# Layer trunk of gated DeltaNet and GLA on one core: the recurrence's output and the gate computed transposed

## The chip, the core and the metric

One core of one Trainium2 chip runs the whole program. The metric is device time in microseconds (us), the median of several executions. The kernel before took 3088.72 us, the median of three runs (3087.71 to 3092.79).

## What is computed

Two layers over 2048 tokens of width 1024, all in float32. Layer one is a gated DeltaNet with 8 heads (key width 128, value width 256), layer two gated linear attention (GLA) with 4 heads of the same widths. In both, an input projection gives q, k, v and a gate; a recurrence over the tokens gives an output o for each head, which is normalised, gated and projected back:

```python
def gated_rmsnorm(o, w, gate):
    o = o * lax.rsqrt(jnp.mean(o * o, -1, keepdims=True) + RMS_EPS)
    return o * w * jax.nn.silu(gate)

def l2norm(t):
    return t * lax.rsqrt(jnp.sum(t * t, -1, keepdims=True) + L2_EPS)

# layer one: q, k, v pass a causal convolution of 4 taps and SiLU, then q and k pass l2norm
#   S_t = exp(g_t) S_{t-1} (I - beta_t k_t k_t^T) + beta_t v_t k_t^T ;  o_t = S_t q_t
# layer two:
#   S_t = diag(exp(gk_t)) S_{t-1} + k_t^T v_t ;  o_t = q_t S_t
# both:
#   x = layer_norm(ALPHA * x + gated_rmsnorm(o, norm_w, gate) @ w_out)
```

## The kernel before

The tokens come in 4 groups of 512 (`TG`), a group in 4 chunks of 128 (`NC`). A unit of work is one head of one layer over one group: 32 units of layer one and 16 of layer two, 48 in all, in the order of `PHASES`, which sets the second layer's groups between those of the first. Each unit goes through four stages.

`gemms` projects the group's x on the unit's columns: k and q (`kq`), values (`val`) and gate. Each operand is split in a rounded high part and the rest, and every product is made of three (`mm3`: high by high, high by low, low by high), over 8 blocks of 128 input channels. `by_channel` makes the weights stationary and moves 512 tokens; its result has channels on the partitions, two groups of 24 matmuls in PSUM. `by_token` makes 128 tokens stationary and moves the 256 weight columns; its result has tokens on the partitions, four groups of 24 matmuls. The groups are staggered by the `LAGS_C` and `LAGS_T` steps, so that their ends are spread. `kq`, and in layer one `val`, go by channel; the gate, and in layer two `val`, by token. A first head's gate weights carry 16 more columns, from which the decays come. Weight tiles (`wc`, 11 buffers) are loaded raw once (`wraw`, 5 buffers), split in high and low by ScalarE and GpSimd, kept in HBM, and loaded from there for later groups. The gate passes tanh on ScalarE and a product on VectorE into `sg`.

`preps` prepares the chunk matrices of the recurrence. In layer one (`gdn_prep`) k and q are transposed on TensorE, 4 transposes each, and ScalarE sums their squares from PSUM with an accumulator; q's norm is not applied to q but joins the output's norm later (`qn`).

`chains` runs the recurrence over the 4 chunks with the state `S`. For each chunk the output `do` (tokens by 256 values) is the sum of two products in PSUM; `output` squares it on ScalarE with an accumulator (`ssq`) and multiplies it by the gate into `og` on VectorE. At the end GpSimd raises `ssq` to the power -1/2 (`z`), and 8 transposes turn `og` so that values lie on the partitions, each bank of which is split in high and low parts (`oth`, `otl`).

`outs` multiplies these by the output weights, 8 banks of 6 matmuls of 512 columns, and VectorE adds each bank, times `z`, to the row of x (`y`); after a layer's last head comes the layer norm.

No engine order is written by hand. A recorder notes every operation, and `Recorder.place` lays all of them out ahead of time by costs per operation and by rank (recurrence first, then preparation, projection out, GEMM, layer norm); the order of each engine's queue is then fixed. PSUM has 8 banks: 3 for the GEMMs (`psg`), 3 for preparation and outputs (`psc`), one for the recurrence (`psh`) and one for the projection out (`pso`). Since a helper issues everything, all instructions have line 358, and a row is known by its tiles.

Of the kernel before, what the change touches and what calls it, by code (L numbers as in the profile page):

```python
# [16 lines left out]
P = 128  # L17
# [9 lines left out]
ALPHA = 4.0 ** 0.25  # L27
BIG = 1.0e30
NORM = 0.5 * DV ** 0.5 / ALPHA
LEVELS = (1, 2, 4, 8, 16, 32, 64)  # L30

C_ID, C_TRI, C_ONE, C_LO, C_UP, C_BLK, C_LV = 0, 1, 2, 3, 4, 5, 6
N_CST = C_LV + 5


def shape_constants(np):
    i = np.arange(P)[:, None]
    j = np.arange(P)[None, :]
    c = np.zeros((P, N_CST, P), np.float32)
    c[:, C_ID] = i == j  # L40
    c[:, C_TRI] = i <= j
    c[:, C_ONE] = 1.0
# [335 lines left out]
def trunk(ctx, tc, x, xT, w_in1, conv, a_log, dt_bias, nw1, w_out1, w_in2, gk_up, gk_b, nw2, w_out2,  # L378
# [54 lines left out]
    nws = [T(f"nw{k}", [P, 2]) for k in range(2)]  # L433
    gkb = T("gkb", [P, H2])
    mhalf = T("mhalf", [P, NC])
    up = T("up", [80, 512], dt=F32R)
    halo = T("halo", [P, 32, 3])
    S1 = [T(f"S1_{h}", [P, DV]) for h in range(H1)]
# [9 lines left out]
    def setup():  # L448
        sync.dma_start(nalog[:], a_log.unsqueeze(0).broadcast_to([P, H1]))
        sync.dma_start(dtb[:], dt_bias.unsqueeze(0).broadcast_to([P, H1]))  # L450
        sync.dma_start(cst[:].rearrange("p a b -> p (a b)"), consts)
        sync.dma_start(nws[0][:], nw1)
        v.tensor_scalar(nws[0][:], nws[0][:], NORM, None, ALU.mult)
        s.activation(nalog[:], nalog[:], AF.Exp)
        v.tensor_scalar(nalog[:], nalog[:], -1.0, None, ALU.mult)
        v.memset(mhalf[:], -0.5)
        v.tensor_reduce(id16[:], ident.rearrange("p (a b) -> p b a", b=16), mybir.AxisListType.X, ALU.add)
        for t in S1 + S2 + [halo]:
            v.memset(t[:], 0.0)
# [91 lines left out]
        return [(t[:, j, 0, :], t[:, j, 1, :]) for j in range(2)]  # L551

    def gemm(u, specs, group, lags, done):
        xs = u.G["x"]
        d, chunks = [None] * len(lags), {}
        for i in range(KC + lags[-1]):
            for a, lag in enumerate(lags):
# [5 lines left out]
                if a == 0:  # L563
# [40 lines left out]
    class Unit:  # L604
        def __init__(self, at, kind, gi, h):
            self.at, self.kind, self.gi, self.h = at, kind, gi, h
            self.t0 = gi * TG
            self.first, self.last = h == 0, h == (H1, H2)[kind] - 1

        def w_specs(self):  # L610
            h = self.h
            if self.kind == 0:
                gate = [(QKV + h * DV, DV, 0)] + ([(QKV + H1 * DV, 2 * H1, 0)] if self.first else [])
                kq = [(h * P, P, 1024)]
                val = [(2048 + h * DV, DV, 0)]
# [16 lines left out]
    def gemms(u):  # L632
# [11 lines left out]
            rec.rank = R_GEMM  # L644
        specs = u.w_specs()

        def gate(width):
            u.sg = T("sg", [P, NC, DV], 2)
            if u.first:
                u.G["low"] = T("ba", [P, NC, 16])  # L650

            def done(d, n):
                t = T("th", [P, 512], 2)
                s.activation(t[:, :DV], d[:, :DV], AF.Tanh, scale=0.5)
                if u.first:
                    s.copy(u.G["low"][:, n, :], d[:, DV:width])
                v.scalar_tensor_tensor(u.sg[:, n, :], t[:, :DV], 1.0, d[:, :DV], ALU.add, ALU.mult)
# [20 lines left out]
        if u.first and u.at:  # L678
            gate(DV + 16)
        u.kq = T("kq", [P, 2, NC, P], 2)  # L680
        gemm(u, specs["kq"], by_channel, LAGS_C, kq_done)
        if u.at == 0:
            gate(DV + 16)
        u.vt = T("vt", [P, NC, DV], 2)
        if u.kind == 0:
            gemm(u, specs["val"], by_channel, LAGS_C, val_done)
            rec.rank = R_PREP
# [7 lines left out]
        else:  # L695
# [15 lines left out]
    def gdn_logits(G, gi):  # L711
# [28 lines left out]
        mm(d[:, 1, :], C(C_ONE), zz)  # L740
# [9 lines left out]
        row = T("gcT", [H1 * NC, P])  # L750
        s.copy(row[:], dT)
        rows = T(f"gcT_{gi}", [H1 * NC, P], p=dr)
        acts.dma_start(rows[:], row[:])
        G.update(beta=beta, gc=gc, gdec=gl, eg=eg, rows=rows)

    def later_half(a, sz):
# [8 lines left out]
    def gdn_prep(u):  # L765
# [26 lines left out]
        rk = r[:]  # L792
        brk, br2, s1 = (small(k, NC) for k in ("brk", "br2", "s1"))
        v.tensor_scalar(qn[:], ss[:, NC:], 1e-6, P * DV * 1e-6, ALU.add, ALU.mult)
# [166 lines left out]
    def output(u, n, do, og, ssq):  # L961
        jk = T("junk", [P, DV], 1, BF16)
        s.activation(jk[:], do, AF.Square, accum_out=ssq[:, n:n + 1])
        v.tensor_tensor(og[:, n, :], do, u.sg[:, n, :], ALU.mult)

    def gdn_chain(u, og, ssq):
        S, p, kq = S1[u.h], u.prep, u.kq
        eg = u.G["eg"]
        for n in range(NC):
# [6 lines left out]
            mm(d, p["Uf"][:, n], Rt[:])  # L976
            wt = T("wt", [P, DV], 2)
            s.copy(wt[:], d)
            do = PS("c", [P, DV])
            mm(do, p["qd"][:, n], S[:], True, False)  # L980
# [3 lines left out]
            mm(do, p["Bt"][:, n], wt[:], False, True)  # L984
            output(u, n, do, og, ssq)

    def gla_chain(u, og, ssq):
        S, p = S2[u.h], u.prep
        for n in range(NC):
            d = PS("h", [P, DV])  # L990
            mm(d, p["kd"][:, n], u.vt[:, n, :])
            do = PS("c", [P, DV])
            mm(do, p["At"][:, n], u.vt[:, n, :], True, False)
            mm(do, p["qd"][:, n], S[:], False, True)
            v.scalar_tensor_tensor(S[:], S[:], p["el"][:, n:n + 1], d, ALU.mult, ALU.add)
            output(u, n, do, og, ssq)

    def chains(u):
        rec.rank = R_CHAIN
        og, ssq = T("og", [P, NC, DV], 1), small("ssq", NC)  # L1000
        (gdn_chain if u.kind == 0 else gla_chain)(u, og, ssq)
        z = small("z", NC)
        if u.kind == 1:
            rsqrt(z[:], ssq[:], DV * 1e-6)
        else:
            v.tensor_tensor(ssq[:], ssq[:], u.prep["qn"][:], ALU.add)
            rsqrt(z[:], ssq[:], 0.0)
        u.z = z
        u.oT = []
# [133 lines left out]
```

## Time and profile before

| | us |
|---|---|
| median of 3 runs | 3088.72 |
| the profiled execution | 3087.8 |
| its span, first to last instruction | 3086.0 |
| TensorE busy | 3009.3 |
| VectorE busy | 2051.1 |
| ScalarE busy | 1142.8 |
| GpSimd busy | 474.2 |

The mean granted TensorE clock was 0.995. A float32 product shows as two instructions, the three parts of a GEMM product as one each. Matmuls are pipelined: one lasts longer in the records than it holds back the next, so times are better read from one start to the next. Idle time of an engine is told with what ended it.

### The profile page before, as it was taken

The page shows a single profiled execution, that of the slowest core. Times are in us where ns is not written, and L with a number is a line of the kernel's source. Part 1 is how long each engine was busy: PE and PEld are TensorE (multiplying, and loading weights), DVE is VectorE, ACT ScalarE, POOL GpSimd, SP SyncE. Part 2 cuts the span into 40 slices and gives each one's busy share as a digit, 9 for nine tenths or more (in the row PEclk, how much of TensorE's full clock was granted, in tenths as well). Part 3 has the DMA queues.
Part 4 walks back from the last instruction along what each step waited for, and adds up shares of the span by engine and source line. Part 5 has one row for each costly group of instructions (what it writes and reads, how often), then busy time and mean ns, then how long its engine had stood idle before and what let it go on. Part 6 is the DMA issues. An engine that isn't in the chain of part 4 may idle for free. (4 is left out here: it accounts for less than half of the span.)

```text
span 3086.0 us, 51431 instructions
## 1 busy us (share of the span) xinstructions
PE 3009.3 (98%) x18430; PEld 2580.0 (84%) x18430; DVE 2051.1 (66%) x4810; ACT 1142.8 (37%) x3075; POOL 474.2 (15%) x820
## 2 busy tenths in 40 slices
PE   9999999999999999999999999999999999999997
PEld 7778888778888878988888888998888888889886
DVE  7777777866666685576675667447666667646645
ACT  5444445433223454433332344223333333422421
POOL 5433333510000232210000000001000000000000
PEclk9999999999999999999999999999999999999999
DMA  6565667764455567674445445547444544655542
GB/s 197 167 206 186 208 217 229 220 218 124 136 164 174 156 207 269 212 240 154 126 144 180 144 157 194 171 153 251 132 134 152 161 134 149 224 168 186 189 143 94
DMA packets 428272, 545.50 MB, mean 177 GB/s; under 512 B 38720, under 2 KB 364608, under 8 KB 415984
## 3 DMA queue, kind: packets, MB, share of 16 engines
q1 hardware_dynamic: 414000, 524.32, 54.1%
q10 hardware_dynamic: 14016, 17.90, 1.8%
q8 instruction: 145, 2.38, 0.3%
q14 instruction: 111, 0.91, 0.1%
HBM read 414.89 MB, written 127.21 MB: 176 GB/s over the span
## 5 line engine op out<-in xcount | busy, mean ns | idle before, releaser
L358 PE MATMUL psg<-xh,wc 128*128 128x512 f32 x2560 | 898.1, 414 | 6.4 <-ACT xh L358 2.8
L358 PE MATMUL psg<-wc,xh 128*128 128x256 f32 (+1 forms) x4096 | 807.4, 290 | 10.8 <-POOL wc L358 3.9
L358 PEld LDWEIGHTS psg<-wc,xh 128*128 128x128 f32 x4096 | 652.8, 189 | 36.5 <-POOL wc L358 5.6
L358 PE MATMUL psg<-wc,xl 128*128 128x256 f32 (+1 forms) x2048 | 586.7, 289 | 0.0
L358 PEld LDWEIGHTS psg<-xh,wc 128*128 128x128 f32 x2560 | 478.2, 189 | 104.3 <-ACT xh L358 3.9
L358 PE MATMUL psg<-xl,wc 128*128 128x512 f32 x1280 | 526.8, 412 | 0.1
L358 PE MATMUL pso<-wo,oth 128*128 128x512 f32 x1472 | 471.1, 400 | 6.0 <-DVE y L358 5.3
L358 DVE SCALAR_TENSOR_TENSOR y<-pso,z,y 128x512 f32<-128x512 f32 x368 | 274.6, 746 | 179.7 <-PE pso L358 175.4
L358 PEld LDWEIGHTS psg<-wc,xl 128*128 128x128 f32 x2048 | 386.8, 190 | 7.6
L358 POOL TENSOR_TENSOR wc<-wraw,wc 128x256 fp32r<-128x256 f32 (+1 forms) x336 | 278.1, 845 | 420.4 <-ACT wc L358 373.9
L358 DVE SCALAR_TENSOR_TENSOR acc<-pb,taps,acc 128x512 f32<-128x512 f32 x384 | 307.3, 802 | 51.7 <-ACT acc L358 44.1
L358 PEld LDWEIGHTS pso<-wo,oth 128*128 128x128 f32 x1472 | 258.0, 188 | 63.8 <-DVE y L358 17.1
L358 PE MATMUL pso<-wo,otl 128*128 128x512 f32 x736 | 293.1, 398 | 0.5 <-DVE otl L358 0.3
L358 PEld LDWEIGHTS psg<-xl,wc 128*128 128x128 f32 x1280 | 241.6, 189 | 48.4 <-DVE xl L358 1.9
L358 ACT ACTIVATE th<-psg 128x256 f32<-128x256 f32 (+1 forms) x256 | 108.2, 436 | 465.2 <-PE psg L358 434.6
L358 ACT ACTIVATE junk<-psc 128x128 bf16<-128x128 f32 (+1 forms) x448 | 144.6, 323 | 240.5 <-PE psc L358 135.2
L358 ACT COPY pb<-psg 128x512 f32<-128x512 f32 x128 | 74.9, 585 | 303.6 <-PE psg L358 279.4
L358 PEld LDWEIGHTS pso<-wo,otl 128*128 128x128 f32 x736 | 138.3, 188 | 32.1 <-DVE otl L358 2.0
L358 POOL COPY halo<-pb 128x3 f32<-128x3 f32 x128 | 29.9, 233 | 879.7 <-ACT pb L358 878.9
L358 DVE SCALAR_TENSOR_TENSOR sg<-th,psg 128x256 f32<-128x256 f32 x192 | 80.0, 417 | 127.6 <-ACT th L358 111.7
L358 ACT CAST wc<-wraw 128x256 fp32r<-128x256 f32 (+1 forms) x336 | 126.9, 407 | 90.7 <-DMA wraw<-in_w_in 77.4
L358 DVE SCALAR_TENSOR_TENSOR S<-S,eg,psh 128x256 f32<-128x256 f32 x128 | 61.1, 477 | 125.1 <-PE psh L358 124.4
(169 smaller groups left out, 4282.0 us busy)
## 6 DMA issues: line engine op xcount, KB each, us to landing
wc<-wk SPq DMA_DIRECT2D x776, 256.0 KB
wo<-wok SPq DMA_DIRECT2D x70, 1024.0 KB
wk<-wc SPq DMA_DIRECT2D x272, 256.0 KB
wraw<-in_w_in SPq DMA_DIRECT2D x336, 128.0 KB
wok<-wo SPq DMA_DIRECT2D x24, 1024.0 KB
Arep<-blk SPq DMA_DIRECT2D x32, 512.0 KB
woraw<-in_w_out SPq DMA_DIRECT2D x48, 256.0 KB
wc<-wk SPq DMA_DIRECT2D x40, 272.0 KB
```

What stands on the lines that cost most here:

```text
L358: tc.keep_in_program_order(op.call(*[real(a) for a in op.args], **{k: real(a) for k, a in op.kw.items()}))
```

## The change

The gate is computed by channel in all units but five (the first head of layer one in each group, and the very last unit, which keep the old form: `by_tok`). The output of the recurrence is computed with values on the partitions: for each of the two products of a chunk, the two halves of the value operand are stationary and the 128-token operand moves. The result, squared and gated, needs no transposing; `og` is split directly. The squares are kept whole (`sq`); the two halves are added, in layer one q's squares (scaled) are added to them, the sum is split, and two products with a matrix of ones give every partition the sum over all of them; a product with the identity and four accumulating copies bring the sums back to tokens on partitions. So q is no longer transposed for its norm. In layer two a first head computes its values first, with the 16 more columns, and the gate last. By-token groups with kept weights are computed in two passes of two chunks each, with the weights loaded for each pass. There is one weight buffer and one raw buffer fewer, and the matrix of ones is made on the chip.

```diff
-W_BUFS, RAW_BUFS, X_RAW_BUFS = 11, 5, 4
+W_BUFS, RAW_BUFS, X_RAW_BUFS = 10, 4, 4
...
+    ones = T("ones", [P, P], dt=F32R)
...
     def gemm(u, specs, group, lags, done):
+        if len(lags) > 2 and specs[0][3] in kept:
+            for a in range(0, len(lags), 2):
+                passes(u, specs, group, {a: 0, a + 1: LAGS_C[1]}, done)
+        else:
+            passes(u, specs, group, dict(enumerate(lags)), done)
...
+            self.by_tok = kind == 0 and self.first or at + 1 == len(units)
...
-                gate = [(2048 + h * DV, DV, 0)] + ([(3072, 16, 0)] if self.first else [])
+                gate = [(2048 + h * DV, DV, 0)]
                 kq = [(h * P, P, 512)]
-                val = [(1024 + h * DV, DV, 0)]
+                val = [(1024 + h * DV, DV, 0)] + ([(3072, 16, 0)] if self.first else [])
...
-            gemm(u, specs["gate"], by_token(width), LAGS_T, done)
+            if u.by_tok:
+                gemm(u, specs["gate"], by_token(DV + 16 if u.first else DV), LAGS_T, done)
+            else:
+                gemm(u, specs["gate"], by_channel, LAGS_C, done)
...
+        if u.kind == 1 and u.first:
+            gemm(u, specs["val"], by_token(DV + 16), LAGS_T, val_done)
+        if u.kind == 0 and u.first and u.at:
+            gate()
...
-        if not u.first:
-            gate(DV)
+        if u.kind == 1 or not u.first:
+            gate()
...
-        for m in range(2):
+        for m in range(2 if u.by_tok else 1):
             d = PS("c", [P, NC, P])
             transposes(d, lambda n: kq[:, m, n], NC)
...
+        else:
+            c = slice(n * P, (n + 1) * P)
+            s.activation(sq[:, :2, c], do, AF.Square)
+            v.tensor_tensor(u.og[:, :, c], do, u.sg[:, :, c], ALU.mult)
...
+    def accumulate(u, do, steps, first, last):
+
+        for i, (tok, val) in enumerate(steps):
+            f, l = first and i == 0, last and i == len(steps) - 1
+            if u.by_tok:
+                mm(do, tok, val, f, l)
+            else:
+                for j in range(2):
+                    mm(do[:, j, :], val[:, j * P:(j + 1) * P], tok, f and j == 0, l and j == 1)
...
-        for j in range(2):
-            d = PS("c", [P, NC, P])
-            transposes(d, lambda n: og[:, n, j * P:(j + 1) * P], NC)
-            hi = T("oth", [P, NC, P], 2, F32R)
-            lo = T("otl", [P, NC, P], 2, F32R)
-            split(hi[:], lo[:], d)
-            u.oT.append((hi, lo))
...
+        v.tensor_tensor(sq[:, 0], sq[:, 0], sq[:, 1], ALU.add)
+        if u.kind == 0:
+            s.activation(sq[:, 1], flat(u.kq[:, 1]), AF.Square, scale=Q_NORM ** 0.5)
+            v.tensor_tensor(sq[:, 0], sq[:, 0], sq[:, 1], ALU.add)
+        sqh, sql = (T(k, [P, TG], 2, F32R) for k in ("oth", "otl"))
+        split(sqh[:], sql[:], sq[:, 0])
+        d = PS("c", [P, TG])
+        mm(d, ones[:], sqh[:], True, False)
+        mm(d, ones[:], sql[:], False, True)
+        hl = parts()
         for j in range(2):
+            split(flat(hl[j][0][:]), flat(hl[j][1][:]), u.og[:, j])
+            u.oT.append(hl[j])
+        v.tensor_tensor(sq[:, 0].rearrange("p (n t) -> p n t", n=NC), d.rearrange("p (n t) -> p n t", n=NC),
+                        bc(ident, 1, NC), ALU.mult)
+        for n in range(NC):
+            jk = T("junk", [P, DV], 1, BF16)
+            s.activation(jk[:, :P], sq[:, 0, n * P:(n + 1) * P], AF.Copy, accum_out=ssq[:, n:n + 1])
+        rsqrt(z[:], ssq[:], DV * 1e-6 if u.kind else Q_NORM * 1e-6)
```

## Rows read from the trace of the kernel before

**Rows 1.**** The page's busy time, share of the span and instruction count of each engine (PE is the TensorE matmul, PEld its weight load, DVE VectorE, ACT ScalarE, POOL GpSimd).

```profile
PE 3009.3 (98%) x18430; PEld 2580.0 (84%) x18430; DVE 2051.1 (66%) x4810; ACT 1142.8 (37%) x3075; POOL 474.2 (15%) x820
```

**Rows 2.**** The page's 40 equal slices of the span: busy tenths of TensorE, and the clock that it was granted.

```profile
PE   9999999999999999999999999999999999999997
...
PEclk9999999999999999999999999999999999999999
```

**Rows 3.**** Busy time by stretch. Columns: stretch, its length, then busy us (and instructions) of PE, PEld, DVE, ACT and POOL, granted clock, DMA share and GB/s.

```profile
0.00:580.00 580.00, 556.87 (x3210) 462.06 (x3211) 435.00 (x969) 273.74 (x796) 224.87 (x329) 0.99 0.65 201
580.00:1140.00 560.00, 544.47 (x3250) 457.99 (x3250) 387.65 (x939) 206.88 (x573) 89.03 (x161) 1.00 0.55 170
...
1440.00:1900.00 460.00, 457.51 (x2781) 388.73 (x2780) 310.15 (x781) 156.14 (x436) 29.62 (x79) 1.00 0.48 149
...
3060.00:3086.00 26.00, 10.01 (x43) 7.62 (x41) 21.49 (x36) 0.00 (x0) 4.11 (x8) 0.77 0.21 82
```

**Rows 4.**** Who TensorE waited for over the whole span: us in total, times, longest.

```profile
PE psg L358 <- DVE acc L358: 8.7, 9, 2.2
PE psc L358 <- ACT junk L358: 6.5, 10, 1.5
PE pso L358 <- DVE y L358: 5.3, 13, 0.9
...
PE psg L358 <- POOL wc L358: 3.9, 5, 1.8
...
PE psg L358 <- DMA wc<-wk: 1.3, 2, 0.6
```

**Rows 5.**** Timeline of TensorE in the gate's GEMM of a unit of layer one (by token): first and last triple of a stretch in which nothing else stands. Columns: start us, length us, engine, line, operation, out<-in, shapes, how many were merged.

```profile
1678.98 0.41 PE L358 MATMUL psg<-wc,xh 128*128 128x256 f32 x2
...
1688.21 0.40 PE L358 MATMUL psg<-wc,xh 128*128 128x256 f32 x2
```

**Rows 6.**** Timeline of TensorE in a GEMM by channel: first and last triple of such a stretch.

```profile
2129.50 0.62 PE L358 MATMUL psg<-xh,wc 128*128 128x512 f32 x2
...
2144.72 0.64 PE L358 MATMUL psg<-xh,wc 128*128 128x512 f32 x2
```

**Rows 7.**** Timeline of TensorE in the recurrence of layer one (two products, then output transposes), and sixteen passes of layer two's products between halves of small blocks.

```profile
127.83 0.59 PE L358 MATMUL psh<-S,kq 128*128 128x256 f32 x2
128.26 0.59 PE L358 MATMUL psc<-S,qd 128*128 128x256 f32 x2
128.69 0.82 PE L358 MATMUL psc<-cst,og 128*128 128x128 f32 x6
...
1100.10 1.99 PE L358 MATMUL psc<-D 128*128 128x64 f32 x16
```

**Rows 8.**** Groups of TensorE instructions by form over the whole span: count, busy us, mean ns of one, idle us before them and who ended it.

```profile
L358 PE MATMUL psc<-S,qd 128*128 128x256 f32 x384 | 117.3, 387 | 0.2
...
L358 PE MATMUL psc<-D 128*128 128x64 f32 x512 | 63.2, 269 | 2.1 <-DVE D L358 2.1
L358 PE MATMUL psc<-cst,og 128*128 128x128 f32 x384 | 61.3, 274 | 1.4 <-DVE og L358 0.9 <-ACT Gb L358 0.3
...
L358 PE MATMUL psc<-cst,kq 128*128 128x128 f32 x256 | 38.2, 276 | 0.0
```

**Rows 9.**** Groups of VectorE instructions by form, columns as in rows 8.

```profile
L358 DVE TENSOR_TENSOR og<-psc,sg 128x256 f32<-128x256 f32 x192 | 81.1, 423 | 24.9 <-ACT junk L358 22.2
L358 DVE SCALAR_TENSOR_TENSOR sg<-th,psg 128x256 f32<-128x256 f32 x192 | 80.0, 417 | 127.6 <-ACT th L358 111.7 <-ACT ba L358 15.4
...
L358 DVE TENSOR_TENSOR otl<-psc,oth 128x512 fp32r<-128x512 f32 x96 | 61.7, 683 | 29.5 <-ACT oth L358 29.1
...
L358 DVE TENSOR_TENSOR xl<-xraw,xh 128x512 fp32r<-128x512 f32 x64 | 44.2, 700 | 10.3 <-ACT xh L358 10.1
...
L358 DVE SCALAR_TENSOR_TENSOR vt<-th,psg 128x512 f32<-128x512 f32 x64 | 41.9, 683 | 17.2 <-ACT th L358 16.8
```

**Rows 10.**** Groups of ScalarE instructions by form, columns as in rows 8.

```profile
L358 ACT ACTIVATION_READ_ACCUMULATOR junk<-psc 128x1 f32 x448 | 88.1, 197 | 0.0
...
L358 ACT ACTIVATE th<-psg 128x256 f32<-128x256 f32 x192 | 73.2, 383 | 391.2 <-PE psg L358 363.6 <-DVE Xt L358 12.3 <-DVE y L358 8.9
...
L358 ACT ACTIVATE junk<-psc 128x128 bf16<-128x128 f32 x256 | 71.4, 279 | 37.3 <-DVE kd L358 26.4 <-PE psc L358 4.3 <-PE psh L358 0.7
...
L358 ACT CAST xh<-xraw 128x512 fp32r<-128x512 f32 x64 | 39.2, 621 | 22.3 <-PE psg L358 11.2 <-DMA xraw<-x2T 7.7 <-DMA xraw<-in_xT 1.9
L358 ACT ACTIVATE th<-psg 128x512 f32<-128x512 f32 x64 | 35.3, 597 | 74.0 <-PE psg L358 71.0 <-DVE X L358 2.9
```

**Rows 11.**** Two stretches with much DMA traffic, columns as in rows 3.

```profile
2660.00:2665.00 5.00, 3.79 (x32) 3.40 (x31) 3.02 (x8) 1.90 (x4) 0.00 (x0) 1.00 1.06 399
...
1900.00:1920.00 20.00, 19.23 (x163) 18.13 (x161) 14.45 (x36) 10.40 (x20) 1.28 (x2) 1.00 0.99 324
```

**Rows 12.**** The loads of kept weight tiles as SP issued them: count, ns of the issue (least, median, most), first and last start.

```profile
L358 SPq DMA_DIRECT2D wc<-wk x816: 319/518/1583, 617.3 to 3040.9; - x164
```

**Rows 13.**** Timeline of TensorE where the gate of a layer-two unit ends, the next unit's product by channel starts, and the output projection starts.

```profile
2010.59 0.28 PE L358 MATMUL psg<-wc,xl 128*128 128x256 f32 x1
2010.70 0.40 PE L358 MATMUL psg<-xh,wc 128*128 128x512 f32 x1
...
2014.38 0.63 PE L358 MATMUL pso<-wo,oth 128*128 128x512 f32 x2
```

More of the change, by code (lines that the diff above doesn't have):

```diff
@@ L456, in setup @@
         v.memset(mhalf[:], -0.5)
+        t = T("th", [P, 512], 2)
+        v.memset(t[:, :P], 1.0)
+        s.copy(ones[:], t[:, :P])
         v.tensor_reduce(id16[:], ident.rearrange("p (a b) -> p b a", b=16), mybir.AxisListType.X, ALU.add)
@@ L553, in gemm, with passes @@
     def gemm(u, specs, group, lags, done):
+        if len(lags) > 2 and specs[0][3] in kept:
[3 more added lines that the diff above has]
+            passes(u, specs, group, dict(enumerate(lags)), done)
+    def passes(u, specs, group, lags, done):
         xs = u.G["x"]
-        d, chunks = [None] * len(lags), {}
-        for i in range(KC + lags[-1]):
-            for a, lag in enumerate(lags):
+        d, chunks = {}, {}
+        for i in range(KC + max(lags.values())):
+            for a, lag in lags.items():
                 kc = i - lag
@@ L645, in gemms, with gate @@
         specs = u.w_specs()
[L647 to L650, printed above, removed]
+        if u.first:
+            u.G["low"] = T("ba", [P, NC, 16])
+        def gate():
+            if u.by_tok:
+                u.sg = T("sg", [P, NC, DV], 2)
+            else:
+                u.sg = T("sg", [P, 2, TG], 2)
             def done(d, n):
+                w = DV if u.by_tok else TG
                 t = T("th", [P, 512], 2)
[L654 to L657, printed above, removed]
-            gemm(u, specs["gate"], by_token(width), LAGS_T, done)
+                s.activation(t[:, :w], d[:, :w], AF.Tanh, scale=0.5)
+                if u.by_tok and u.first:
+                    s.copy(u.G["low"][:, n, :], d[:, DV:DV + 16])
+                v.scalar_tensor_tensor(u.sg[:, n, :], t[:, :w], 1.0, d[:, :w], ALU.add, ALU.mult)
+            if u.by_tok:
+                gemm(u, specs["gate"], by_token(DV + 16 if u.first else DV), LAGS_T, done)
+            else:
+                gemm(u, specs["gate"], by_channel, LAGS_C, done)
         def kq_done(d, m):
@@ L676, in val_done @@
                 s.copy(u.vt[:, m, :], d[:, :DV])
-        if u.first and u.at:
-            gate(DV + 16)
+                if u.first:
+                    s.copy(u.G["low"][:, m, :], d[:, DV:DV + 16])
+        u.vt = T("vt", [P, NC, DV], 2)
+        if u.kind == 1 and u.first:
+            gemm(u, specs["val"], by_token(DV + 16), LAGS_T, val_done)
+        if u.kind == 0 and u.first and u.at:
+            gate()
         u.kq = T("kq", [P, 2, NC, P], 2)
@@ L694, in gemms @@
             rec.rank = R_GEMM
-        else:
+        elif not u.first:
             gemm(u, specs["val"], by_token(DV), LAGS_T, val_done)
-        if not u.first:
-            gate(DV)
+        if u.kind == 1 or not u.first:
+            gate()
     def short_conv(d, blk):
@@ L739, in gdn_logits @@
         mm(d[:, 0, :], C(C_TRI), zz)
-        mm(d[:, 1, :], C(C_ONE), zz)
+        mm(d[:, 1, :], ones[:].bitcast(F32), zz)
         gc, gl = T("gc", [P, 2, H1, NC], 2), T("gdec", hn, 2)
@@ L749, in gdn_logits @@
         pe.transpose(dT, gcf[:, 0, :], ident)
-        row = T("gcT", [H1 * NC, P])
-        s.copy(row[:], dT)
+        row = T("Gb", [P, TG])[:H1 * NC, :P]
+        s.copy(row, dT)
         rows = T(f"gcT_{gi}", [H1 * NC, P], p=dr)
-        acts.dma_start(rows[:], row[:])
+        acts.dma_start(rows[:], row)
         G.update(beta=beta, gc=gc, gdec=gl, eg=eg, rows=rows)
@@ L959, in preps, with output, out_bank, gdn_chain @@
         (gdn_prep if u.kind == 0 else gla_prep)(u)
[L961 to L966, printed above, removed]
+    def output(u, n, do, sq):
+        if u.by_tok:
+            jk = T("junk", [P, DV], 1, BF16)
+            s.activation(jk[:], do, AF.Square, accum_out=sq[:, n:n + 1])
+            v.tensor_tensor(u.og[:, n, :], do, u.sg[:, n, :], ALU.mult)
+        else:
[5 more added lines that the diff above has]
+            f, l = first and i == 0, last and i == len(steps) - 1
+            if u.by_tok:
+                mm(do, tok, val, f, l)
+            else:
+                for j in range(2):
+                    mm(do[:, j, :], val[:, j * P:(j + 1) * P], tok, f and j == 0, l and j == 1)
+    def out_bank(u):
+        return PS("c", [P, DV] if u.by_tok else [P, 2, P])
+    def gdn_chain(u, sq):
         S, p, kq = S1[u.h], u.prep, u.kq
@@ L983, in gdn_chain, with gla_chain @@
             v.scalar_tensor_tensor(S[:], S[:], eg[:, 1, u.h, n:n + 1], d, ALU.mult, ALU.add)
-            mm(do, p["Bt"][:, n], wt[:], False, True)
-            output(u, n, do, og, ssq)
-    def gla_chain(u, og, ssq):
+            accumulate(u, do, [(p["Bt"][:, n], wt[:])], False, True)
+            output(u, n, do, sq)
+    def gla_chain(u, sq):
         S, p = S2[u.h], u.prep
@@ L991, in gla_chain @@
             mm(d, p["kd"][:, n], u.vt[:, n, :])
-            do = PS("c", [P, DV])
-            mm(do, p["At"][:, n], u.vt[:, n, :], True, False)
-            mm(do, p["qd"][:, n], S[:], False, True)
+            do = out_bank(u)
+            accumulate(u, do, [(p["At"][:, n], u.vt[:, n, :]), (p["qd"][:, n], S[:])], True, True)
             v.scalar_tensor_tensor(S[:], S[:], p["el"][:, n:n + 1], d, ALU.mult, ALU.add)
-            output(u, n, do, og, ssq)
+            output(u, n, do, sq)
     def chains(u):
@@ new lines, in chains, with parts @@
+        z, ssq = small("z", NC), small("ssq", NC)
+        u.z, u.oT = z, []
+        def parts():
+            return [[T(k, [P, NC, P], 2, F32R) for k in ("oth", "otl")] for j in range(2)]
+        if u.by_tok:
+            hl = parts()
+            u.og = T("og", [P, NC, DV], 1)
+            chain(u, ssq)
+            if u.kind == 0:
+                v.tensor_tensor(ssq[:], ssq[:], u.prep["qn"][:], ALU.add)
+            rsqrt(z[:], ssq[:], DV * 1e-6 if u.kind else 0.0)
+            for j in range(2):
+                d = PS("c", [P, NC, P])
+                transposes(d, lambda n: u.og[:, n, j * P:(j + 1) * P], NC)
+                split(hl[j][0][:], hl[j][1][:], d)
+                u.oT.append(hl[j])
+            return
@@ new lines, in chains @@
+        u.og = T("og", [P, 2, TG], 1)
+        sq = T("sq", [P, 2, TG])
+        chain(u, sq)
+        v.tensor_tensor(sq[:, 0], sq[:, 0], sq[:, 1], ALU.add)
+        if u.kind == 0:
+            s.activation(sq[:, 1], flat(u.kq[:, 1]), AF.Square, scale=Q_NORM ** 0.5)
[4 more added lines that the diff above has]
+        mm(d, ones[:], sqh[:], True, False)
```

29 lines of the change are left out of this document (11 added, 18 removed).

## The prediction

> **What bounds the kernel now.** I read the engines' busy time first, then the slices, then where TensorE stands still. TensorE is busy for 3009.3 of 3086.0 us, VectorE for 2051.1, ScalarE for 1142.8, GpSimd for 474.2 [rows 1]. The reader is to see that only one engine is near the span, and in every slice of it: the TensorE line is all nines, and its clock is at nine tenths or more throughout [rows 2]. Busy alone doesn't prove it, since matmuls overlap in the records, so next come stretches: 0 to 580 us leave TensorE idle for 23.1 us, 580 to 1140 for 15.5, but 1440 to 1900 for only 2.5; the last 26 us hold 16 idle ones, the tail of the last layer norm [rows 3]. The list of who TensorE waits for is short and spread out: the largest entry is 8.7 us for a convolution's result, then 6.5 for a PSUM bank that ScalarE is squaring from, and weights cost 3.9 (GpSimd's split) and 1.3 (a load) [rows 4]. So the sum goes by TensorE: what one matmul pushes the next one back by (its spacing, not its duration), times the number of matmuls that come or go. Other engines matter only where they make TensorE wait.
>
> **The spacings.** A gate product by token moves 256 columns: triples start at 1678.98 and, 26 triples later, at 1688.21, so 9.23 us / 78 = 0.1183 us each [rows 5]. A product by channel moves 512: 2129.50 to 2144.72 is 22 triples, 15.22 / 66 = 0.2306 us [rows 6]. In the recurrence float32 products of 256 columns start at 127.83 and 128.26 and the next thing at 128.69, so 0.43 each [rows 7]; one is two passes (384 instructions for 192 products [rows 8]), so 0.215 a pass. Six transposes take 0.82 us together and one lasts 0.274 [rows 7, 8]: (0.82 - 0.274) / 5 = 0.109.
>
> **The change part by part.** There are 48 units (32 of the first layer, 16 of the second). By token stay the four first heads of layer one and the very last unit; 43 units change: 28 of layer one, 15 of layer two.
>
> Gate: 43 units trade 96 matmuls of 256 columns for 48 of 512. 96 x 0.1183 = 11.357, 48 x 0.2306 = 11.069; 43 x 0.288 = 12.4 us less.
>
> Transposes of the output: 8 in each of 43 units, 344 x 0.109 = 37.5 us less. Transposes of q: 4 in each of 28 units, 112 x 0.109 = 12.2 us less. They were not idle filler: the idle time before them is 1.4 and 0.0 us [rows 8].
>
> The transposes are where a rule would speak loudest. Their records last 274 and 276 ns [rows 8], yet six of them pass in 0.82 us [rows 7]. The Trainium skill, "TensorE: Matmul & The Clock Gate", section "Part 4: PE-mode transpose", gives some 275 ns for one in a kernel; the durations here agree, but by it as a price the 456 transposes would save 125 us and the sum below would be -112 us instead of -36. The spacing decides, so that price has no place in my sum.
>
> Output products: 43 x 4 chunks x 2 products of two passes are 688 passes x 0.215 = 147.9 us. They become 1376 passes of 128 columns, each with its own 128-column weight load. No such pass is in the trace. From below, a transpose (128 columns, one load): 0.109, so 150.0. From above, a pass that moves only 64 columns under a 128-column load, 16 in 1.99 us with one lasting 0.269 [rows 7, 8]: 0.115, so 157.9. A cost below nothing is excluded, since the same columns move. I take the middle, 0.112: 154.1, or 6.2 us more (2.1 to 10.0), since it has the columns of the one and the two-pass load of the other.
>
> Ones products: two of 512 columns in 43 units, 86 x 0.2306 = 19.8 us more.
>
> Sum on TensorE: -12.4 - 37.5 - 12.2 + 6.2 + 19.8 = -36.1 us.
>
> **Beside the path.** VectorE per changed unit: the gate's four operations of 0.417 become two like the 0.683 one [rows 9], -0.3 us; the output's four stay at 0.423; the splits read SBUF (0.700) for PSUM (0.683), nothing; new are the sum of the two halves of squares, the low part of its split and, in layer one, the adding of q's squares, 0.700 each, and the masked product from PSUM at 0.683. That is about +2.5 in layer one and +1.8 in layer two, 97 us in all: VectorE goes from 66% to 70%, and TensorE's work covers it. ScalarE loses q's squares (4 x (0.279 + 0.197)) and four accumulator reads in layer one, and trades four tanh of 0.383 for two of 0.597; it gains two passes of about 0.62 and four sums of the diagonal at about 0.5 [rows 10]. Its 63% idle time covers that. If the cover failed, each microsecond would be paid 43 times.
>
> New wait: the ones products stand in TensorE's fixed order behind squares, sum and split, and the GEMM's matmuls stand behind them. The nearest row is the output transposes, which stood at the same place and waited 1.4 us in 48 units [rows 8]. I take nothing, with 5 us as the upper end. It could be below nothing: without q's transposes one bank fewer is held while ScalarE squares, and that wait is 6.5 us now [rows 4]. The splits now read the gated output itself, so its single buffer, and the two buffers of split halves (the sum of squares passes through one of them too), are held until the unit before is projected; the next unit's output comes tens of microseconds later, so nothing.
>
> Moved: in a first head of layer two the gate goes from the front to the end and its 16 extra columns go to the values, whose group goes first. The same matmuls, loads and copies are issued in another order; SP and TensorE are past the place only once in four groups. Nothing, within 2 us either way. The set-up gains a memset and a copy and loses a constant: nothing.
>
> Buffers: weight tiles go from 11 to 10, raw ones from 5 to 4. By channel a tile is free three steps after its load instead of eleven, so the waits for weights (3.9 + 1.3 [rows 4]) may halve or double: 0, from -3 to +5.
>
> Two passes: 15 by-token groups with kept weights (12 values in layer two, two gates in layer one, the last gate) load their weights twice, 120 more loads of 256 KB. 16 tiles are 4.19 MB in 96 x 0.1183 = 11.36 us, 369 GB/s. The queue delivered 399 GB/s over 5 us, but 324 over 20 us at a share of 0.99 [rows 11]. At 399 nothing is late; at 324 a group takes 12.95 us and 15 groups lose 24 us. SP needs 0.518 us for an issue [rows 12], 16 fit. I take 0: six tiles run ahead and TensorE has other work between.
>
> The Trainium skill, "DMA: Bandwidth & Descriptors", section "Specifications", speaks against this part: some 358 GB/s from HBM for one core. By it a group takes 11.7 us, 15 groups lose 5 us and the sum would be -31. The 399 of the trace is above that limit, so I don't charge it.
>
> **The rivals.** (1) Weights late: as just worked out, plus the 5 us for fewer buffers: 3052.6 + 24 = 3077, at most some 3082. For it speaks the 0.99 share; against it that TensorE waited 1.3 us for such loads in all. (2) Stalls fall as well: half of the idle time before 1140 us (38.6 [rows 3]) goes with fewer banks and smoother weights: 3053 - 19 = 3034. Against it: most of those waits end on parts that the change leaves alone. (3) Slower: in layer two the gate comes last and every output chunk now waits for all of it. From the last gate matmul to the first projection it is 0.597 tanh + 0.683 + 4 x 0.423 + 0.700 + 0.621 + 0.700 for the split sum + 0.461 ones + 0.621 + 0.700 for the last split = 6.8 us, where 3.8 stand now (2010.59 to 2014.38 [rows 13]). Today the next unit's products fill it without a gap (from 2010.70). If they can't start, since the gate's halves hold two of three PSUM banks, up to 6.8 x 15 = 102 us are lost; the change turns slower from 2.4 us in each of the 15 units, and at half of the full price it ends at 3052.6 + 51 = 3104. Against it: the next products need one bank at first, and they alone last 11 us.
>
> **How the numbers follow.** The profiled execution took 3087.8 us, 0.9 under the median of 3088.7. 3087.8 - 36.1 = 3051.7; with the 0.9, 3052.6. Forecast 0.67, rival 1 0.12, rival 2 0.11, rival 3 0.10. About 0.2% (6.2 us) is what a measurement of this kernel can tell from no change. Nearly all of the first three lies below 3082.5: faster 0.83, same 0.07, slower 0.10. The range takes in the ends of the unknown costs and most of rivals 1 and 2, and leaves out rival 3: 3030 to 3082.
>
> **What would show it.** In the changed kernel's profile: 384 output transposes fall to 40, TensorE's busy time falls by about 36 us and its idle time stays near 77; output passes stand 0.109 to 0.115 us apart; VectorE's share is about 70%. Waits of TensorE for weight loads well over 10 us would show rival 1; gaps of some microseconds after each layer-two gate would show rival 3. The prediction is wrong if passes of 128 columns cost over 0.13, or if the idle time grows by as much as the matmuls save.

## The result and the profile after

The changed kernel took 3058.83 us, median of four runs (3053.76 to 3058.95), against 3088.81 before: a ratio of 0.9897, interval 0.9879 to 0.9914. Run once more beside other kernels it gave 3057.03 us and 0.9896 (0.9883 to 0.9910). That is 32 us less by the ratio (27 to 37 by its interval), where 36.1 were forecast. One order of instructions, executed again, spreads from 3052.7 to 3061.2 us, so a few microseconds between two medians tell nothing.

The page of the profiled execution (3058.86 us, span 3057.1), its engine line and the slices of TensorE and VectorE, answers to [rows 1, 2]:

```profile
PE 2976.7 (97%) x16684; PEld 2469.4 (81%) x16684; DVE 2125.1 (70%) x4826; ACT 1187.1 (39%) x3009; POOL 500.1 (16%) x848
...
PE   8999999999999999999999999999999999999997
...
DVE  6887788866766696586677668548677676755755
```

TensorE's busy time falls by 32.6 us and its idle time is 80.4 us where it was 76.7. VectorE is up by 74.0 us (97 were counted), to the 70% of the forecast.

Busy time is not work alone. When the changed kernel was run once more (`a_again`, called the repeat below), its profiled execution (3052.66 us, span 3050.9) had 6.0 us less busy time for the same instructions, and the same idle time, 80.2 us:

```profile
PE 2970.7 (97%) x16684; PEld 2465.4 (81%) x16684; DVE 2125.0 (70%) x4826; ACT 1186.3 (39%) x3009; POOL 499.7 (16%) x848
```

What differs is TensorE's clock: the mean granted was 0.993 in the first and 0.995 in the second, as before the change. One stretch in both executions, the first one above, columns as in [rows 3]:

```profile
632.00:650.00 18.00, 16.20 (x109) 13.05 (x108) 4.77 (x15) 8.49 (x27) 1.28 (x2) 0.81 0.87 310
632.00:650.00 18.00, 15.32 (x112) 12.17 (x111) 7.66 (x22) 8.47 (x29) 1.27 (x2) 1.00 0.86 298
```

In the first TensorE stood still for 1.48 us in one piece and then ran at 1.2 GHz, the lower of its two levels, for some 7 of the 18 us; in the second it stood still for longer in all (2.68 for 1.80 us), in pieces of at most 1.31, and stayed at 2.4 GHz. So a busy time is good to some 6 us. Busy time times mean clock, an estimate of the work alone, is 2994 us before and 2956 in both profiles after: some 38 us less, where 36.1 were worked out. The stretches of the first profile, columns as in [rows 3]:

```profile
0.00:580.00 580.00, 550.84 (x2919) 441.24 (x2920) 448.58 (x971) 282.35 (x774) 234.00 (x340) 0.99 0.65 200
580.00:1140.00 560.00, 549.41 (x3012) 447.92 (x3010) 408.95 (x950) 214.44 (x553) 93.11 (x167) 0.99 0.56 173
1140.00:1440.00 300.00, 287.66 (x1597) 240.00 (x1597) 199.19 (x423) 123.05 (x301) 67.01 (x100) 0.98 0.71 232
1440.00:1900.00 460.00, 458.04 (x2595) 381.17 (x2594) 328.09 (x796) 166.96 (x427) 35.73 (x85) 1.00 0.52 160
...
3031.10:3057.10 26.00, 10.08 (x42) 7.45 (x40) 21.50 (x36) 0.00 (x0) 4.12 (x8) 0.76 0.21 81
```

The middle (1440 to 1900) has as little idle time as before, 2.0 us. Idle time still sits in the stretches in which weights are first loaded: 29.2 us from 0 to 580, 10.6 to 1140, 12.3 to 1440. Who TensorE waits for, as in [rows 4]:

```profile
PE psg L358 <- ACT xraw L358: 9.0, 8, 3.5
PE pso L358 <- DVE y L358: 8.4, 15, 1.5
PE psg L358 <- ACT wc L358: 6.2, 4, 3.9
PE psc L358 <- ACT junk L358: 4.8, 8, 1.0
PE psg L358 <- DVE acc L358: 4.3, 4, 2.0
...
PE psg L358 <- DMA wc<-wk: 3.8, 6, 1.9
PE psg L358 <- POOL wc L358: 2.2, 5, 1.0
...
PE psg L358 <- DVE sg L358: 0.5, 1, 0.5
```

No wait became large. The wait for the convolution's result halved (8.7 to 4.3) and the one for the bank that ScalarE squares from fell (6.5 to 4.8); those for a split raw weight (ScalarE's `wc`, 2.1 to 6.2), for weight loads (1.3 to 3.8), for the projection's single bank (5.3 to 8.4) and for `xraw`, the copy that carries x to layer two (3.0 to 9.0), rose. The three waits for weights add up to 12.2 us where they were 7.3; in the repeat they are 9.8. For the gate's product (`sg`) TensorE waits 0.5 us in all.

The new output passes, on TensorE's timeline in layer two:

```profile
1102.20 0.61 PE L358 MATMUL psc<-D,vt 128*128 128x128 f32 x4
1102.64 0.61 PE L358 MATMUL psc<-qd,S 128*128 128x128 f32 x4
1103.09 1.06 PE L358 MATMUL psc<-D,vt 128*128 128x128 f32 x8
1103.98 0.60 PE L358 MATMUL psh<-vt,kd 128*128 128x256 f32 x2
```

Sixteen passes of 128 columns take 1103.98 - 1102.20 = 1.78 us, 0.111 each, between the two bounds of [rows 7, 8]. TensorE's groups by form, columns as in [rows 8]:

```profile
L358 PE MATMUL psc<-qd,S 128*128 128x128 f32 x688 | 106.5, 277 | 0.1
...
L358 PE MATMUL psc<-D,wt 128*128 128x128 f32 x448 | 68.0, 274 | 0.0
...
L358 PE MATMUL psc<-D,vt 128*128 128x128 f32 x240 | 36.0, 278 | 0.2 <-ACT sq L358 0.2
...
L358 PE MATMUL psc<-cst,kq 128*128 128x128 f32 x144 | 22.9, 284 | 0.0
...
L358 PE MATMUL psc<-oth,ones 128*128 128x512 f32 x43 | 17.6, 410 | 0.5 <-ACT oth L358 0.5
L358 PE MATMUL psc<-otl,ones 128*128 128x512 f32 x43 | 17.4, 404 | 0.0
...
L358 PE MATMUL psc<-cst,og 128*128 128x128 f32 x40 | 6.4, 275 | 0.8 <-DVE og L358 0.7
```

The counts are those of the working: 688 + 448 + 240 = 1376 passes, 86 ones products, 40 output transposes left. None of them has idle time worth naming ahead of it, so the ones products, which wait for squares, sum and split, are placed late enough. VectorE's three new operations, columns as in [rows 9]:

```profile
L358 DVE TENSOR_TENSOR sq<-sq 128x512 f32<-128x512 f32 x71 | 48.6, 685 | 3.2 <-ACT sq L358 2.9
...
L358 DVE TENSOR_TENSOR otl<-sq,oth 128x512 fp32r<-128x512 f32 x43 | 30.6, 711 | 15.9 <-ACT oth L358 14.2 <-PE pso L358 1.5
...
L358 DVE TENSOR_TENSOR sq<-psc,cst 128x512 f32<-128x512 f32 x43 | 29.4, 685 | 2.5 <-PE psc L358 2.5
```

### The profile page after: what moved, and what is told of

It is laid out like the page before. It is cut to its first block, busy times and chain, and to the rows that moved or that the text cites. A ratio compares the mean times of both kernels' runs of the same rounds, so it can differ in the third digit from the quotient of the medians.

```text
span 3057.1 us, 48020 instructions
## 1 busy us (share of the span) xinstructions
PE 2976.7 (97%) x16684; PEld 2469.4 (81%) x16684; DVE 2125.1 (70%) x4826; ACT 1187.1 (39%) x3009; POOL 500.1 (16%) x848
## 5 line engine op out<-in xcount | busy, mean ns | idle before, releaser
L358 PE MATMUL psg<-xh,wc 128*128 128x512 f32 x3936 | 1358.1, 409 | 14.5 <-ACT xh L358 4.1
L358 PEld LDWEIGHTS psg<-xh,wc 128*128 128x128 f32 x3936 | 734.7, 189 | 174.5 <-POOL wc L358 5.6
L358 PE MATMUL psg<-xl,wc 128*128 128x512 f32 x1968 | 797.7, 406 | 0.1
L358 PEld LDWEIGHTS psg<-xl,wc 128*128 128x128 f32 x1968 | 372.1, 189 | 74.9 <-DVE xl L358 1.6
L358 PE MATMUL psg<-wc,xh 128*128 128x256 f32 (+1 forms) x1344 | 267.8, 291 | 5.9 <-ACT wc L358 3.9
L358 PEld LDWEIGHTS psg<-wc,xh 128*128 128x128 f32 x1344 | 216.0, 190 | 13.9 <-ACT wc L358 4.4
L358 ACT ACTIVATE th<-psg 128x512 f32<-128x512 f32 (+1 forms) x170 | 94.8, 572 | 303.0 <-PE psg L358 300.7
L358 PE MATMUL psg<-wc,xl 128*128 128x256 f32 (+1 forms) x672 | 192.1, 289 | 0.2 <-DVE xl L358 0.2
L358 ACT CAST wc<-wraw 128x256 fp32r<-128x256 f32 (+1 forms) x336 | 127.0, 405 | 97.4 <-DMA wraw<-in_w_in 80.2
L358 DVE SCALAR_TENSOR_TENSOR sg<-th,psg 128x512 f32<-128x512 f32 (+1 forms) x106 | 67.1, 634 | 125.9 <-ACT th L358 111.0
L358 ACT ACTIVATE D<-D 128x512 f32<-128x512 f32 x160 | 98.6, 629 | 141.7 <-DVE D L358 118.2
```

The lines of the kernel that those rows point to most:

```text
L358: tc.keep_in_program_order(op.call(*[real(a) for a in op.args], **{k: real(a) for k, a in op.kw.items()}))
```

## The experiments

The theory: the time follows TensorE's work, which changes by spacings times counts, and everything that was added elsewhere stays covered. The rivals: late weights (doubled loads, fewer buffers), and stalls that the gate's old form or q's bank had caused. Each kernel is the changed one with one edit, or the kernel before with one part alone. Ratios are to the kernel before; differences to the changed kernel are differences of ratios (from 0.9897) times 3089 us. The ranges given with them join both kernels' intervals: such a difference is good to 6 to 8 us. Idle is the span less TensorE's busy time.

| kernel | ratio (95%) | TensorE busy, idle | against the changed kernel | forecast by the theory |
|---|---|---|---|---|
| `b_fewer_buffers` | 1.0038 (1.0026 to 1.0051) | 3016.0, 84.0 | - | 0 to the kernel before |
| `a_one_pass` | 0.9883 (0.9868 to 0.9899) | 2975.0, 76.1 | -4 | 0 |
| `a_gate_by_token` | 0.9987 (0.9978 to 0.9996) | 2989.5, 95.1 | +28 | +12.4 |
| `a_q_transposed` | 0.9926 (0.9914 to 0.9939) | 2983.6, 83.4 | +9 | +12.2 |
| `a_transposes_back` | 0.9994 (0.9984 to 1.0004) | 3008.4, 79.0 | +30 | +37.5 |
| `a_ones_twice` | 0.9933 (0.9919 to 0.9946) | 2986.8, 78.2 | +11 | +19.8 |
| `a_gate_first` | 0.9900 (0.9885 to 0.9915) | 2978.8, 80.9 | +1 | 0 |
| `a_squares_stationary` | 0.9936 (0.9924 to 0.9949) | 2988.8, 76.9 | +12 | +1 to +19 |
| `a_again` | 0.9896 (0.9883 to 0.9910) | 2970.7, 80.2 | 0 | 0 |
| `a_fewer_still` | 1.0018 (1.0008 to 1.0027) | 2992.0, 108.5 | +37 | 0 |
| `a_one_pass_11` | 0.9884 (0.9871 to 0.9898) | 2968.7, 83.9 | -4 | -6 |
| `a_one_pass_raw5` | 0.9891 (0.9872 to 0.9909) | 2967.7, 84.7 | -2 | -10 to -16 |

**The output's transposes put back** (`a_transposes_back`).

```diff
+        for j in range(2):
+            unread = PS("c", [P, NC, P])
+            transposes(unread, lambda n: u.og[:, j, n * P:(n + 1) * P], NC)
         hl = parts()
```

> The changed kernel with 8 transposes of the gated output in each of the 43 changed units put back; they go to a PSUM bank that nothing reads. Theory (TensorE's work adds up one for one): 344 x 0.109 = 37.5 us more than 3059: 3096 us. Rival (they fit in gaps of TensorE, and the gain came from elsewhere): 3059 to 3075 us.

Some 30 us came back (24 to 36), and as busy time of TensorE, 2976.7 to 3008.4, not as idle time (80.4 to 79.0):

```profile
PE 3008.4 (97%) x17028; PEld 2503.9 (81%) x17028; DVE 2122.3 (69%) x4826; ACT 1188.1 (38%) x3009; POOL 505.9 (16%) x848
```

So the largest term of the sum is work on TensorE and lay in no gap. By time it is some four fifths of its listed size.

**q's transposes put back** (`a_q_transposed`).

```diff
-        for m in range(2 if u.by_tok else 1):
+        for m in range(2):
...
-        if u.by_tok:
+        if True:
             v.tensor_scalar(qn[:], ss[:, NC:], 1e-6, Q_NORM, ALU.add, ALU.mult)
```

> The changed kernel with q's transposes and their squares put back in the 28 units (their result is used by nothing). Theory: 112 transposes x 0.109 = 12.2 us more: 3071 us. Rival (what they cost is the PSUM bank that is held while ScalarE squares): 20 us more or above, 3079 us, with the wait of TensorE for that bank at double its 4.8 us.

9 us (2 to 16): the theory's term, and below the rival's 20; the wait for ScalarE's bank fell to 2.8 us instead of doubling. What q's transposes cost is their own work, as far as this can tell; the 34 us that ScalarE did more (1187.1 to 1221.4) cost nothing that shows.

**The ones products issued twice** (`a_ones_twice`).

```diff
         mm(d, ones[:], sql[:], False, True)
+        mm(d, ones[:], sqh[:], True, False)
+        mm(d, ones[:], sql[:], False, True)
```

> The changed kernel with the two ones products issued twice (the second pair overwrites the first with the same sums). Theory: 86 x 0.2306 = 19.8 us more: 3079 us. Rival (the wait for the split sum is what the ones products cost, and a second pair runs in its shadow): within 5 us of 3059.

11 us (4 to 18), between the two: neither number holds. The engine line of this kernel:

```profile
PE 2986.8 (97%) x16770; PEld 2481.7 (81%) x16770; DVE 2123.7 (69%) x4826; ACT 1188.7 (39%) x3009; POOL 500.3 (16%) x848
```

Busy time rose by 10.1 us (16.1 against the repeat), idle time fell by 2.2. The 86 added matmuls are in the trace. Why they cost some 11 us and not 19.8 isn't settled: part of it is the clock, 0.994 here for 0.993, and part may be waiting that the profile counts within busy time and that this order doesn't have.

**The gate by token** (`a_gate_by_token`).

```diff
-                gemm(u, specs["gate"], by_channel, LAGS_C, done)
+                passes(u, specs["gate"], by_token(DV), dict(enumerate(LAGS_T)), done)
...
-                u.sg = T("sg", [P, 2, TG], 2)
+                whole = T("sg", [P, 2 * TG], 2)
+                u.sg = whole.rearrange("p (j t) -> p j t", j=2)
+                by_n = whole.rearrange("p (n e) -> p n e", n=NC)
```

> The changed kernel with the gate of all units by token, one pass, old lags; the transposed output then multiplies the same gate values in a wrong order (the output is not the reference's). Theory: 43 units x 96 matmuls of 256 columns for 48 of 512, 43 x 0.288 = 12.4 us more: 3071 us. Rival (the gate's form matters by its stalls, four evacuations and weights held longer): 25 us more or above, 3084 us, with TensorE's idle time up by over 10 us.

28 us (22 to 34). The engine line, and the waits of TensorE that grew:

```profile
PE 2989.5 (97%) x18748; PEld 2586.0 (84%) x18748; DVE 2130.9 (69%) x4912; ACT 1195.3 (39%) x3095; POOL 503.2 (16%) x848
```

```profile
PE psg L358 <- ACT wc L358: 9.7, 5, 3.8
...
PE psg L358 <- DVE sg L358: 6.8, 4, 5.3
PE psg L358 <- POOL wc L358: 5.9, 4, 4.4
```

Busy time is up by 12.8 us (18.8 against the repeat, which has the higher clock), where the theory has 12.4 for the columns, and idle time by 14.7 beside it. The clearest part of that is PSUM banks that wait for the gate's product (0.5 to 6.8). The waits for raw weights are longer too (6.2 to 9.7 for ScalarE's half of the split, 2.2 to 5.9 for GpSimd's), but the first is 11.2 us in `a_q_transposed`, which leaves weights alone, so its rise alone tells little. The columns and the stalls have about half each, and theory and rival both hold. With the buffers of the changed kernel, the gate's new form is worth twice its columns.

**The buffers** (`b_fewer_buffers`, `a_fewer_still`). The first is the kernel before with the changed kernel's numbers of buffers, the second the changed kernel with one less of each.

```diff
-W_BUFS, RAW_BUFS, X_RAW_BUFS = 11, 5, 4
+W_BUFS, RAW_BUFS, X_RAW_BUFS = 10, 4, 4
```

> The kernel before with 10 weight tiles for 11 and 4 raw ones for 5, nothing else. Theory (TensorE's work sets the time, the cover holds): the same work, 3089 us within 3. Rival (weights come late): each tile by token is held for eleven steps, so the waits of TensorE for weights, 3.9 + 2.1 + 1.3 us before, at least double: 3096 us or more.

```diff
-W_BUFS, RAW_BUFS, X_RAW_BUFS = 10, 4, 4
+W_BUFS, RAW_BUFS, X_RAW_BUFS = 9, 3, 4
```

> The changed kernel with one weight tile and one raw tile fewer still (9 and 3). Theory (with the gate by channel a tile is free after three steps, so the buffers no longer bind): within 4 us of the changed kernel. Rival (a buffer costs what it cost the kernel before): 11 us more, 3070 us or above.

The first lost 12 us (8 to 16, against the kernel before) with not one matmul more. Of the rival's three waits for weights ScalarE's grew from 2.1 to 8.1 and the loads' from 1.3 to 4.3, while GpSimd's fell from 3.9 to 1.7: 7.3 us became 14.1, just short of the doubling that it named. The wait for the gate's product grew from 2.8 to 6.0:

```profile
PE psg L358 <- ACT wc L358: 8.1, 6, 2.9
PE psg L358 <- DVE sg L358: 6.0, 3, 5.3
...
PE psg L358 <- DMA wc<-wk: 4.3, 4, 1.8
...
PE psg L358 <- POOL wc L358: 1.7, 4, 1.1
```

Other waits fell: idle time rose by 7.3 us in all, and busy time by 6.7. The order of instructions is a new one as well, and what that alone is worth was not measured apart; `a_gate_first` below, which changes the order and neither the buffers nor the work, moved by 1 us.

The second lost 37 us (31 to 44), and the theory that the new gate makes buffers unimportant fell. One wait stands out, 6.2 us grown to 36.5:

```profile
PE psg L358 <- ACT wc L358: 36.5, 20, 5.3
```

Its stretches, columns as in [rows 3], show when:

```profile
0.00:580.00 580.00, 543.25 (x2839) 431.35 (x2840) 423.82 (x938) 270.56 (x727) 220.66 (x321) 0.98 0.62 193
580.00:1140.00 560.00, 542.24 (x2947) 440.90 (x2947) 400.30 (x937) 218.16 (x572) 93.50 (x171) 0.99 0.55 170
1140.00:1440.00 300.00, 275.81 (x1523) 230.73 (x1522) 199.73 (x404) 119.53 (x288) 75.86 (x106) 0.97 0.74 237
1440.00:1900.00 460.00, 458.57 (x2582) 377.94 (x2582) 317.44 (x783) 164.14 (x434) 32.35 (x84) 1.00 0.50 152
```

Against the changed kernel TensorE's busy time is short by 7.6, 7.2 and 11.9 us in the first three stretches and equal in the fourth. Raw weights come through ScalarE and GpSimd only there. The profiled execution took 43.4 us more than the changed kernel's: 28.1 of them are idle time, and 15.3 are busy time of the same 16684 matmuls, at a mean granted clock of 0.988 where it was 0.993. The stalls were paid twice, once as idle time and once by the lower clock. Which of the two tiles it is, raw or split, this pair can't say.

**One pass** (`a_one_pass`), and with a buffer back (`a_one_pass_11`, `a_one_pass_raw5`).

```diff
-        if len(lags) > 2 and specs[0][3] in kept:
-            for a in range(0, len(lags), 2):
-                passes(u, specs, group, {a: 0, a + 1: LAGS_C[1]}, done)
-        else:
-            passes(u, specs, group, dict(enumerate(lags)), done)
+        passes(u, specs, group, dict(enumerate(lags)), done)
```

> The changed kernel, but its by-token groups with kept weights run in one pass with the four old lags, so the 120 second loads go. Theory: the same 16 tiles' worth of matmuls, 3059 us within 3. Rival (the doubled loads are late): 5 to 24 us come back, 3035 to 3054 us, and the waits of TensorE for weight loads (3.8 us in the changed kernel) vanish.

```diff
-W_BUFS, RAW_BUFS, X_RAW_BUFS = 10, 4, 4
+W_BUFS, RAW_BUFS, X_RAW_BUFS = 11, 4, 3
```

> The changed kernel in one pass, with 11 weight tiles (one buffer for raw x given up for it). Theory: 3053 us, as with 10, since the layer-one gates no longer hold tiles. Rival (the by-token groups that are left want the eleventh tile): 5 us less or more, 3048 us or below.

```diff
-W_BUFS, RAW_BUFS, X_RAW_BUFS = 10, 4, 4
+W_BUFS, RAW_BUFS, X_RAW_BUFS = 10, 5, 3
```

> The changed kernel in one pass with 10 weight tiles and the fifth raw tile back (one buffer for raw x given up for it). Theory (what the buffers cost is the fourth to fifth raw tile, in the stretches where weights come raw): TensorE's wait for ScalarE's copy of raw weights falls from 5.2 to some 2 us and 4 to 10 us come back, 3043 to 3049 us. Rival (the raw tile costs only below four): 3053 us as with four.

In one pass the wait for weight loads falls from 3.8 to 1.2 us:

```profile
PE psg L358 <- ACT wc L358: 5.2, 3, 3.1
...
PE psg L358 <- DMA wc<-wk: 1.2, 5, 0.3
```

The medians are 3053.38, 3053.32 and 3055.28 us, the lowest of the study. But the intervals overlap that of the changed kernel, and the changed kernel's second profile has a span of 3050.9 us, as short as the 3051.1 in one pass. That the second loads cost 2 to 5 us is likely and not shown. Neither the eleventh weight tile nor the fifth raw tile brought anything more that shows; in the latter the wait for ScalarE's copy stayed, against its theory:

```profile
PE psg L358 <- ACT wc L358: 5.1, 4, 3.6
```

Each of the two gave up a buffer for raw x, and the wait for `xh`, the high part of x that ScalarE makes from it, rose (3.8 us in one pass, 6.4 and 5.4 here), so a small gain may be hidden. As far as these runs tell, ten and four tiles suffice in the changed kernel, and the steep price lies on the step to nine and three.

**The gate first in layer two** (`a_gate_first`).

```diff
+        early = u.kind == 1 and not u.first and not u.by_tok
-        if u.kind == 0 and u.first and u.at:
+        if u.kind == 0 and u.first and u.at or early:
             gate()
...
-        if u.kind == 1 or not u.first:
+        if (u.kind == 1 or not u.first) and not early:
             gate()
```

> The changed kernel with the gate ahead of k, q and values in the 11 later-head units of layer two that had it last. Theory (the next unit's products cover the wait for the whole gate): 3059 us within 4. Rival (outputs that wait for all of the gate hold up TensorE): at least 0.5 us in each comes back, 3053 us or less.

0.9900, the same: nothing came back in the 11 units. With the 0.5 us that TensorE waits for `sg` in the changed kernel, outputs that wait for the whole gate hold nobody up.

**The sums of squares turned round** (`a_squares_stationary`). The edit also raises the cost by which `Recorder.place` lays out products of few columns (the first two lines).

```diff
-                op.cost = mov / 2.25 + 4.5
+                op.cost = max(mov / 2.25 + 4.5, 60)
...
-        mm(d, ones[:], sqh[:], True, False)
-        mm(d, ones[:], sql[:], False, True)
+        for n in range(NC):
+            mm(d[:, n], sqh[:, n * P:(n + 1) * P], ones[:, :4], True, False)
+            mm(d[:, n], sql[:, n * P:(n + 1) * P], ones[:, :4], False, True)
...
-        v.tensor_tensor(sq[:, 0].rearrange("p (n t) -> p n t", n=NC), d.rearrange("p (n t) -> p n t", n=NC),
-                        bc(ident, 1, NC), ALU.mult)
-        for n in range(NC):
-            jk = T("junk", [P, DV], 1, BF16)
-            s.activation(jk[:, :P], sq[:, 0, n * P:(n + 1) * P], AF.Copy, accum_out=ssq[:, n:n + 1])
+        s.copy(ssq[:], d[:, :, 0])
```

> The changed kernel with the sums of squares turned round: each chunk's split squares are stationary and four columns of ones move, so the sums come out with tokens on the partitions, and the masked product (VectorE 0.683 us) and four accumulating copies (ScalarE) per unit go. TensorE has 8 short products for two of 0.2306 us; no row has their spacing, 0.06 to 0.112 each, so 0.48 to 0.90 for 0.46. Theory (only TensorE's work counts): 3059 + 43 x (0.02 to 0.44) = 3060 to 3078 us. Rival (the added VectorE and ScalarE work shows up as waits of TensorE): 5 us or more come back, 3054 us or less if the short products cost 0.06.

VectorE and ScalarE lost 27 and 62 us of work (2097.9 and 1125.2 busy), and the kernel became 12 us slower (5 to 19). The short products on TensorE's timeline:

```profile
203.10 0.25 PE L358 MATMUL psc<-ones,oth 128*128 128x4 f32 x1
203.22 0.25 PE L358 MATMUL psc<-ones,otl 128*128 128x4 f32 x1
...
203.66 0.25 PE L358 MATMUL psc<-ones,otl 128*128 128x4 f32 x1
203.78 0.47 PE L358 MATMUL psg<-xh,wc 128*128 128x512 f32 x1
```

From 203.10 to 203.78 six of them take 0.68 us, 0.113 each, for four columns. Eight at this spacing are 0.90 us for the 0.46 of two ones products, 43 x 0.44 = 19 us of TensorE's work at most. More work on TensorE cost time, as the theory has it. The rival's number stood on short products of 0.06, which they aren't; between 19 us listed and 12 measured, relief of the covered engines may have given up to some 7 us, and this edit doesn't separate the two.

**The changed kernel again** (`a_again`).

> The changed kernel once more, on the chip of the two beside it: 3059 us within 5.

It repeated.

## Why the prediction was right

**The bound** held. Whatever was put on TensorE cost time, in four of five such edits as its busy time alone or for the most part (the gate by token added idle time as well). ScalarE's 34 us more in `a_q_transposed` cost nothing that shows; what less work on VectorE and ScalarE gives was not measured apart, and is small at most.

**The spacings** held: output passes 0.111 (0.112 forecast, 0.109 to 0.115 the bounds), counts as worked out. At 0.111 the output products cost some 5 us more where 6.2 were listed; no run has them alone. The Trainium skill, "TensorE: Matmul & The Clock Gate", section "Part 4: PE-mode transpose", would as a price have made the 344 output transposes worth some 95 us, an estimate from its some 275 ns; putting them back cost 30, so the spacing was the right reading, and the page's figure is a duration.

**The sum** was 36.1 for 32 measured, and 36.1 lies inside the measured interval (27 to 37). By the profiles' spans it is 28.9 us in one execution and 35.1 in the repeat. TensorE's idle time was taken as unchanged and rose by 3.7 us (3.5 in the repeat), and the clock, which the sum left out, moves an execution by some 6 us. The additions came out below their listed sizes by time: transposes 30 of 37.5, ones products 11 of 19.8, q's 9 of 12.2, each good to 6 or 7 us. So a microsecond of listed TensorE work may be worth somewhat less than one of time on this kernel; that some of what is added falls into waits that are there anyway is argued, not shown. Each edit also makes a new order of the whole program, and the idle time moves a few microseconds with it; the two can't be told apart here.

**The buffers** came out as the forecast had them, but its halves are larger than its range. "0, from -3 to +5" was taken for fewer tiles and their earlier release together, and the waits for weights rose by 4.9 us (2.5 in the repeat). By themselves the fewer tiles cost 12 us (8 to 16) on the kernel before, and the old gate in the changed kernel costs some 15 us beyond its columns. Those two fit one loss seen from both ends: with the old gate the smaller buffers cost 12 to 15 us, and the gate by channel makes it go away. The working named the reason (a tile is free after three steps instead of eleven) but not the size, so that the two cancel is in part luck; at nine and three tiles they no longer do.

**Two passes** were taken at nothing. The wait for loads rose by 2.5 us (1.7 in the repeat), and the three kernels in one pass came out 2 to 4 us faster, each good to 6 to 8 us. Rival 1 in its size of 24 us is excluded.

**Rival 3** is excluded by the 0.5 us that TensorE waits for the gate's product, and by the gate's place making no difference in 11 of its 15 units; **rival 2** by idle time that did not fall.

## What to carry to other kernels

Where one engine is busy throughout, price an edit by what one instruction pushes the next back by, read from a stretch in which nothing else stands, and not by its duration; here the whole sum came out at some 0.9 of its size, and single terms put back at 0.56 to 0.80, each within 6 to 7 us. Before two busy times are compared, compare the clocks: the same instructions differed by 6 us. A matmul with the operands exchanged costs the same columns, and what makes it worth doing is the transposes that it saves. Try a buffer count by itself before it is given away: on the kernel before one tile of each kind showed no work and no large wait, yet was worth 12 us, a third of this gain; on the changed kernel the next one was worth 37.

## What the runs showed of the hardware

With a fresh weight load of 128 columns, few moving columns cost about as much as 256 of split or 128 of float32 operands. Split products stood 0.113 us apart with 4 columns and 0.118 with 256 [rows 5]; float32 passes 0.115 with 64 [rows 7, 8] and 0.111 with 128. With 64 weight columns and the same 64 moving ones eight passes take 0.68 us, and one lasts 0.228:

```profile
174.26 0.68 PE L358 MATMUL psc<-U,D 128*64 128x64 f32 x8
```

```profile
L358 PE MATMUL psc<-U,D 128*64 128x64 f32 x256 | 21.7, 228 | 0.0
```

(0.68 - 0.228) / 7 = 0.065 us. So the weight load's columns set the floor, and a product with few columns should make the long operand the moving one. The Trainium skill, "TensorE: Matmul & The Clock Gate", section "LDWEIGHTS (loading the stationary operand)", gives the columns over 1.2 as nanoseconds, an estimate of 107 for 128; the spacings here are 4 to 8 more.
